# Two 512-channel gates ahead of the dilated queries and keys in a hybrid decoder layer

## The chip, the cores and the metric

The kernel runs on one core of one Trainium2 chip. The metric is the device time of one execution in microseconds. Three runs of the kernel before took 474.70, 476.15 and 476.85 us, so the median is 476.15 us.

## What is computed

One post-norm decoder layer for 256 positions of 1024 channels, all in float32. The mixer projects x once into MoBA q, k, v, dilated q, k, v, the three inputs of a short convolution, and three gates; each branch is projected back, weighted by its sigmoid gate and summed:

```python
qa, ka, va, qd, kd, vd, b_gate, c_gate, hc, gate_logits = jnp.split(x @ w_in, split_points, axis=-1)
y_moba = moba_attention(heads(qa, MOBA_HEADS), heads(ka, MOBA_HEADS), heads(va, MOBA_HEADS))
y_conv = b_gate * causal_dwconv(c_gate * hc, w_short_conv)
y_dil = dilated_mixture(heads(qd, DIL_HEADS), heads(kd, DIL_HEADS), heads(vd, DIL_HEADS))
gates = jax.nn.sigmoid(gate_logits).reshape(b, s, N_BRANCH, D_MODEL)
merged = (gates[:, :, 0] * (y_moba @ w_moba_proj)
          + gates[:, :, 1] * (y_conv @ w_conv_proj)
          + gates[:, :, 2] * (y_dil @ w_dil_proj))
return merged @ w_mix_out
```

Behind it come a layer norm, a SwiGLU MLP whose up-projection passes a causal convolution of width 3, and a second layer norm. `w_in` is 1024 x 8448: 768 columns each for dilated q, k and v, and 1024 columns for each of the three gates.

## The kernel before

**Weights.** All weight blocks stand in one list, `blocks`, in the order of their use. A block is 1 MB (128 partitions x 2048 floats) and lands in one of `RAW` = 3 buffers `raw`, by DMAs on SP's queue. `prep` takes the next quarter of a block (a *piece*, 128x512), and `split` makes two operands of it: ScalarE (ACT) casts it to fp32r (L168, or L160 in the first stage), and VectorE (DVE) subtracts that from the original (L169). When the last piece of a block is split, the next block's DMA is issued. Pieces may be made up to `LEAD` = 10 ahead of use; they lie in a pool `b` of 61 buffers, which serves nearly all other intermediate tiles too.

**Products.** `mm3` makes each product of three fp32r matmuls (L229, L230, L231). `project` makes 256 channels as two halves of 128 channels x 256 positions: the weight is loaded, x streams, 24 matmuls of 256 columns a half, and the result lies in one of three PSUM banks `acc`. `by_tokens` makes 512 channels for the two halves of positions: x is loaded, the weight streams, 48 matmuls of 512 columns into two `acc` banks. `tick` runs between: it makes further pieces, hands the finished bank to its consumer (`queries`, `keys`, a sigmoid), and takes one step from the list `side`, in which the attention's steps and `small_weights` wait. Each engine's instructions run in the order written by a scheduler.

**The first stage.** `first_products` runs while x and the first two blocks arrive, one 128-row step k at a time, with transposes of x (L222) between; it makes the queries of dilated groups 0 and 1 (four accumulators, 96 matmuls of 256 columns, L499). Then come the queries of group 2 and the keys of all three groups (`project`), dilated v, and the rest: MoBA, the short convolution, and, for each half d of the 1024 channels, three gates by `by_tokens` with a sigmoid (L580) and the merge of the three branches.

**The small rows.** `small_loads` fetches the convolution weights and bias as rows of 128 floats (12 rows, and 4 x 44 rows). `small_weights` turns them with five PE transposes (L484, L486) into one PSUM tile and copies them out on DVE (L487, L488). It is the fifth entry of `side` while the keys are projected. The short convolution reads `sconv` first, behind the dilated v and the MoBA v; `fconv` is for the MLP.

Of the kernel before, what the change touches and what calls it, by code (L numbers as in the profile page):

```python
# [7 lines left out]
F32 = mybir.dt.float32  # L8
# [3 lines left out]
AF = mybir.ActivationFunctionType  # L12
OP = mybir.AluOpType

P = 128
T = 256
D = 1024
KT = D // P
# [8 lines left out]
DIL_Q, DIL_K, DIL_V = 1536, 2304, 3072  # L27
CONV_B, CONV_C, CONV_H = 3840, 4352, 4864
GATE = 5376
# [8 lines left out]
def trunk(ctx: ExitStack, tc, x, w_in, w_short_conv, w_moba_proj, w_dil_proj, w_conv_proj, w_mix_out,  # L38
          ln1_g, ln1_b, w_up, w_ffn_conv, b_ffn_conv, w_down, ln2_g, ln2_b, out):
    nc = tc.nc  # L40
# [12 lines left out]
    def fresh(name):  # L53
        serial[0] += 1
        return f"{name}{serial[0]}"

    def buf(dt=F32, shape=(P, 512)):
        return act.tile(list(shape), dt, tag="b2", name=fresh("b"), bufs=B2)

    def acc(shape=(P, 512)):  # L60
        return ps.tile(list(shape), F32, tag="acc", name=fresh("acc"), bufs=3)
# [8 lines left out]
    def block(*parts):  # L70

        blocks.append(parts)

    def kview(w, c0, c1, k0=0, k1=None):
        k1 = w.shape[0] // P if k1 is None else k1
        return w[k0 * P:k1 * P, c0:c1].rearrange("(k p) c -> p k c", p=P)

    def columns(base, n):
        for b in range(n):
            c = base + 256 * b  # L80
            block(kview(w_in, c, c + 256))

    def wide(base):

        for k in (0, 4):
            block(kview(w_in, base, base + 512, k, k + 4))

    for k in (0, 4):
        block(kview(w_in, DIL_Q, DIL_Q + 512, k, k + 4))
    columns(DIL_Q + 512, 1)  # L90
    columns(DIL_K, 3)
    wide(DIL_V)
    columns(DIL_V + 512, 1)
# [6 lines left out]
    columns(CONV_B, 2)  # L100
    for c in range(0, D, 512):
        for g in range(3):
            wide(GATE + g * D + c)
        block(kview(w_dil_proj, c, c + 512), kview(w_conv_proj, c, c + 512, 0, 2))
        block(kview(w_conv_proj, c, c + 512, 2, 4), kview(w_moba_proj, c, c + 512, 0, 2))
        block(kview(w_moba_proj, c, c + 512, 2, 4))
# [12 lines left out]
    def load_next(between=None):  # L119
        i = len(loads)  # L120
        if i >= len(blocks):
            return
        r = act.tile([P, 2048], F32, tag="raw", name=fresh("raw"), bufs=RAW)
        at = 0
        for p in blocks[i]:
            k, c = p.shape[1:]
            step = 1 if i < 2 else 2 if i == 2 else k
            for k0 in range(0, k, step):
                if between:
                    between(i * 4 + k0)  # L130
                n = step * c
                loading[0] = nc.sync.dma_start(r[:, at:at + n].rearrange("p (k c) -> p k c", c=c), p[:, k0:k0 + step, :])
                at += n
        loads.append(r)
        pieces.extend((r, c, c + 512 == at) for c in range(0, at, 512))

    def prep(n=1):

        for _ in range(n):
            i = len(ready)  # L140
            if i >= min(len(pieces), used[0] + LEAD):
                return
            r, c, last = pieces[i]
            h, l = buf(F32R), buf(F32R)
            split(r[:, c:c + 512], h, l)
            ready.append((h, l))
            if last:
                load_next()

    def take(n):  # L150

        i = used[0]
        assert len(ready) >= i + n, (len(ready), i, n)
        return ready[i:i + n]

    def behind(last, f, *args):
        if last is None:
            return f(*args)
        with tc.issue_after(last.ins):
            return f(*args)  # L160
# [3 lines left out]
    def split(src, h, l):  # L164
        if in_order:
            in_order[0] = behind(in_order[0], nc.scalar.copy, h, src)
        else:
            nc.scalar.copy(h, src)  # L168
        nc.vector.tensor_sub(l, src, h.bitcast(F32))  # L169


    side, late = [], []

    def tick(n, consume=None, ahead=1):


        used[0] += n
        while late:
            late.pop(0)()
        prep(n + ahead)  # L180
        if consume:
            consume()
        if side:
            side.pop(0)()
# [22 lines left out]
    for i in range(RAW):  # L207
        load_next(load_x if i < 2 else None)
# [18 lines left out]
    def mm3(o, ah, al, bh, bl, first, last):  # L227

        nc.tensor.matmul(o, ah, bh, start=first, stop=False)  # L229
        nc.tensor.matmul(o, ah, bl, start=False, stop=False)  # L230
        nc.tensor.matmul(o, al, bh, start=False, stop=last)  # L231
# [15 lines left out]
    def by_tokens(xs, n, consume, ahead=1):  # L247


        o = [acc() for _ in range(2)]  # L250
        for k in range(0, n, 2):
            w = take(2)
            for i in range(2):
                xh, xl = xs(k + i)
                for t in range(2):
                    s = slice(t * P, (t + 1) * P)
                    mm3(o[t], xh[:, s], xl[:, s], *w[i], k + i == 0, k + i == n - 1)
            tick(2, (lambda: [consume(t, o[t]) for t in range(2)]) if k == n - 2 else None, ahead)
# [30 lines left out]
    def queries(store):  # L289

        def consume(c, o):
            q = buf(F32R, (P, 2, T))
            for a in range(2):
                s = HALF[a]
                nc.scalar.copy(q[s, a, :], o[s, :])
            for a in range(2):
                s, n = HALF[a], HALF[1 - a]
                nc.vector.tensor_sub(q[n, a, :], o[s, :], q.bitcast(F32)[s, a, :])  # L298
            store.append(q)
        return consume  # L300
# [145 lines left out]
    def both(*fs):  # L446
        return lambda: [f() for f in fs]
# [41 lines left out]


    dq, dk, dv = [[], [], []], [[], [], []], []
    o = [(acc if c < 2 else att)((P, T)) for c in range(4)]

    def first_products(k, part):

        w = ready[k]
        xt, i = ((xTh, 0), (xTl, 0), (xTh, 1))[part]
        for c in range(4):
            last = nc.tensor.matmul(o[c], w[i][:, c * P:c * P + P], xt[:, k, :], start=k + part == 0,  # L499
                                    stop=k == KT - 1 and i == 1)  # L500
        if part == 2:
            used[0] += 1
            prep(1 if used[0] > 4 else 0)
        return last

    turns = {(0, 0): ((0, 1), (1, 2)), (1, 0): ((2, 4),), (3, 0): ((4, 6),), (5, 0): ((6, 8),)}
    last = None
    for k in range(KT):
        for part in range(3):
            for k0, k1 in turns.get((k, part), ()):  # L510
                last = behind(last, transpose_x, k0, k1)
                prep(k1 - k0)
            if k + part == 0:
                last = behind(last, warmed, 2, 256)
            last = behind(last, first_products, k, part)
    in_order.clear()
    for g in range(2):
        q = queries(dq[g])
        for c in range(2):
            q(c, o[2 * g + c])  # L520
            prep()
    for g in range(2, 3):
        project(queries(dq[g]), ahead=0)
    small_loads()
    side += [lambda: None] * 4 + [small_weights]
    for g in range(3):
        project(keys(dk[g]), ahead=0)
    assert not side
    yd = [buf(F32R, (P, 2, T)) for _ in range(2)]
    p, q = (dilated(c, dq, dk, dv, [t[:, c, :] for t in yd]) for c in range(2))  # L530
    side += [p[0], p[1], p[2], q[0], p[3], p[4], q[1], p[5], q[2], p[6], q[3], q[4], q[5], q[6]]
    dv.extend(project_tokens())
    dv.append(project_tokens_half())
    mv = project_tokens()
# [3 lines left out]
    for b in range(2):  # L538
# [21 lines left out]
        p, q = (moba(c, mq, mk, mv[b], [t[:, c, :] for t in ym]) for c in range(2))  # L560
# [15 lines left out]
    for d in range(2):  # L576
        gs = []
        for g in range(3):
            s = [buf(F32), buf(F32)]
            by_tokens(of_x, KT, lambda t, o: nc.scalar.activation(s[t], o, AF.Sigmoid))  # L580
            gs.append(s)
        assert not side
        h, l = ([buf(F32R, (P, 2, T)) for _ in range(2)] for _ in range(2))

        def turn_m(t, gs=gs, h=h, l=l):
            p = att((P, 4, P))
            for i in range(4):
                nc.tensor.transpose(p[:, i, :], gs[2][t][:, i * P:(i + 1) * P], ident)  # L588
            for i in range(2):
                split(p[:, 2 * i:2 * i + 2, :], h[i][:, :, t * P:(t + 1) * P], l[i][:, :, t * P:(t + 1) * P])  # L590

        for g, n, ys in ((2, 2, [yd]), (1, 4, ycT), (0, 4, ymT)):

            def merge(t, o):
                nc.vector.tensor_mul(gs[g][t], o, gs[g][t])
                if g < 2:
                    nc.vector.tensor_add(gs[2][t], gs[2][t], gs[g][t])

            by_tokens(lambda k: [y[:, k % 2, :] for y in ys[k // 2]], n, merge)
        side += [lambda f=turn_m: f(0), lambda f=turn_m: f(1)]  # L600
        merged.extend(zip(h, l))
# [69 lines left out]
    w = take(4)  # L671
# [16 lines left out]
    def between():  # L688
        passed.append(prep(1))
        if len(passed) == 2:  # L690
            turn_x1(0, 0)
            turn_x1(0, 1)
# [29 lines left out]
    w = take(8)  # L722
    u = []
    for t in range(2):
        o = acc()
        s = slice(t * P, (t + 1) * P)
# [23 lines left out]
    for j in range(2, NJ, 2):  # L750
# [3 lines left out]
        while 2 < j < NJ - 2 and pend:  # L754
            w = take(4)
# [49 lines left out]
```

## Time and profile before

| what | value |
|---|---|
| median of 3 runs | 476.15 us |
| the profiled execution | 475.9 us, of which 474.1 us span |
| TensorE (PE) busy | 463.7 us (98%) |
| VectorE (DVE) busy | 355.5 us (75%) |
| ScalarE (ACT) busy | 268.4 us (57%) |
| mean granted TensorE clock | 0.992 |
| moved by DMA | 83.45 MB, 176 GB/s |

The span is cut into 40 slices in the profile's second part; a busy TensorE there is a sequence of pipelined matmuls, whose rate is read from the distance of their starts, not from their durations. The granted clock is given as a share of 2.4 GHz.

### The profile page before, as it was taken

To read this page: it belongs to the slowest core of one execution; us is meant where nothing else is said; L and a number is where in the kernel's file an instruction comes from. 1 tells how busy PE (TensorE), PEld (TensorE's weight loads), DVE (VectorE), ACT (ScalarE), POOL (GpSimd) and SP (SyncE) were. 2 spreads that over 40 slices of the span, in tenths; PEclk is the share of its full clock that TensorE was granted. 3 is DMA by queue.
4 is the path that set the end of the run, shared out by engine and by line. 5 is a ranking of instruction groups with operands and counts; after the bars stand their busy time and mean duration, and the time that the engine had idled before them with its cause. 6 is when DMAs were issued, how large, how long until landed. Compare 5 with 4: busy or idle time off the path is not lost.

```text
span 474.1 us, 8155 instructions
## 1 busy us (share of the span) xinstructions
PE 463.7 (98%) x3095; PEld 426.3 (90%) x3095; DVE 355.5 (75%) x756; ACT 268.4 (57%) x568; POOL 10.4 (2%) x29
## 2 busy tenths in 40 slices
PE   8989999999999999999999999999999999999993
PEld 6989898999999888888888899999999999999983
DVE  5895998678989944775477966997767686786866
ACT  4894585736667844634463325876565565664710
POOL 1100000010100000000000000000000000000000
PEclk9998999999999999999999999999999999999998
DMA  8963665653544654646554804557455646637202
GB/s 283 325 205 105 197 183 176 224 178 90 178 130 138 187 201 168 220 159 207 191 211 146 266 1 154 201 179 267 157 199 178 198 157 205 225 107 248 105 1 88
DMA packets 57739, 83.45 MB, mean 176 GB/s; under 512 B 1705, under 2 KB 41317, under 8 KB 57701
## 3 DMA queue, kind: packets, MB, share of 16 engines
q1 hardware_dynamic: 57700, 82.94, 52.7%
q8 instruction: 24, 0.39, 0.4%
q14 instruction: 15, 0.11, 0.1%
HBM read 81.89 MB, written 1.05 MB: 175 GB/s over the span
## 4 chain that ended last, share of the span: by engine, by line
PE 94%; DMA 2%; DVE 2%; issue 1%; SPq 0%; ACT 0%; DVEq 0%
PE acc L229 23%; PE acc L231 22%; PE acc L230 22%; PE att L230 7%; PE att L229 7%; PE att L231 7%; PE att L326 2%; PE att L347 1%; DMA b<-in_w_ffn_conv_dram 1%; PE acc L499 1%; PE att L499 1%; DMA xs<-in_x_dram 1%; DVE b L169 1%; DVE b L298 0%; PE att L588 0%
## 5 line engine op out<-in xcount | busy, mean ns | idle before, releaser
L169 DVE TENSOR_TENSOR b<-raw,b 128x512 fp32r<-128x512 f32 x300 | 194.0, 686 | 41.6 <-ACT b L168 38.7
L168 ACT CAST b<-raw 128x512 fp32r<-128x512 f32 x288 | 160.2, 619 | 2.4 <-DMA raw<-in_w_up_dram 2.1
L229 PE MATMUL acc<-x1Th,b 128*128 128x256 f32 x320 | 90.9, 284 | 0.0
L231 PE MATMUL acc<-x1Th,b 128*128 128x256 f32 x320 | 90.6, 283 | 0.0
L230 PE MATMUL acc<-x1Tl,b 128*128 128x256 f32 x320 | 90.5, 283 | 0.0
L229 PE MATMUL acc<-xTh,b 128*128 128x256 f32 x224 | 64.8, 289 | 0.4 <-DVE b L298 0.4
L230 PE MATMUL acc<-xTl,b 128*128 128x256 f32 x224 | 63.9, 285 | 0.0
L231 PE MATMUL acc<-xTh,b 128*128 128x256 f32 x224 | 63.9, 285 | 0.0
L230 PEld LDWEIGHTS acc<-x1Tl,b 128*128 128x128 f32 x320 | 61.4, 192 | 0.1
L229 PEld LDWEIGHTS acc<-x1Th,b 128*128 128x128 f32 x320 | 61.4, 192 | 0.1
L231 PEld LDWEIGHTS acc<-x1Th,b 128*128 128x128 f32 x320 | 61.4, 192 | 0.0
L702 DVE SCALAR_TENSOR_TENSOR b<-acc,fconv,b 128x255 f32<-128x255 f32 x80 | 38.3, 479 | 30.3 <-ACT b L700 29.3
L229 PE MATMUL att<-b,b 128*128 128x512 f32 (+1 forms) x170 | 59.1, 348 | 0.0
L230 PE MATMUL att<-b,b 128*128 128x512 f32 (+1 forms) x170 | 58.9, 347 | 0.0
L231 PE MATMUL att<-b,b 128*128 128x512 f32 (+1 forms) x170 | 58.7, 346 | 0.0
L229 PE MATMUL acc<-b,xTh 128*128 128x512 f32 (+1 forms) x144 | 54.7, 381 | 0.0
L230 PE MATMUL acc<-b,xTh 128*128 128x512 f32 (+1 forms) x144 | 54.4, 378 | 0.0
L231 PE MATMUL acc<-b,xTl 128*128 128x512 f32 (+1 forms) x144 | 54.4, 378 | 0.0
L229 PEld LDWEIGHTS acc<-xTh,b 128*128 128x128 f32 x224 | 43.6, 194 | 0.8 <-PE acc L231 0.6
L230 PEld LDWEIGHTS acc<-xTl,b 128*128 128x128 f32 x224 | 43.6, 195 | 0.0
L231 PEld LDWEIGHTS acc<-xTh,b 128*128 128x128 f32 x224 | 43.5, 194 | 0.0
L700 ACT ACTIVATE b<-acc,fconv 128x256 f32<-128x256 f32 x40 | 22.6, 564 | 28.7 <-PE acc L231 28.6
(118 smaller groups left out, 649.2 us busy)
## 6 DMA issues: line engine op xcount, KB each, us to landing
raw<-in_w_in_dram SPq DMA_DIRECT2D x30, 1024.0 KB, 5.4
raw<-in_w_up_dram SPq DMA_DIRECT2D x22, 1024.0 KB, 5.2
raw<-in_w_down_dram SPq DMA_DIRECT2D x11, 1024.0 KB, 5.0
raw<-in_w_mix_out_dram SPq DMA_DIRECT2D x4, 1024.0 KB, 4.9
raw<-in_w_in_dram SPq DMA_DIRECT2D x12, 256.0 KB, 5.5
raw<-in_w_conv_proj_dram SPq DMA_DIRECT2D x4, 512.0 KB, 4.8
raw<-in_w_moba_proj_dram SPq DMA_DIRECT2D x4, 512.0 KB, 5.1
xs<-in_x_dram SPq DMA_DIRECT2D x4, 256.0 KB, 4.9
```

Source lines behind the costliest of these rows:

```text
L168: nc.scalar.copy(h, src)
L169: nc.vector.tensor_sub(l, src, h.bitcast(F32))
L229: nc.tensor.matmul(o, ah, bh, start=first, stop=False)
L230: nc.tensor.matmul(o, ah, bl, start=False, stop=False)
L231: nc.tensor.matmul(o, al, bh, start=False, stop=last)
L326: nc.tensor.matmul(o, qt, k[i][:, a, :], start=i == 0, stop=i == 1)
L347: nc.tensor.transpose(p[:, i, :], b, ident)
L499: last = nc.tensor.matmul(o[c], w[i][:, c * P:c * P + P], xt[:, k, :], start=k + part == 0, stop=k == KT - 1 and i == 1)
L700: nc.scalar.activation(v, o, AF.Identity, bias=w[3], scale=w[0])
L702: nc.vector.scalar_tensor_tensor(v[:, j:], o[:, :T - j], w[j], v[:, j:], op0=OP.mult, op1=OP.add)
```

## The change

The first stage makes 512 channels of gate 2, by tokens, in place of the queries of groups 0 and 1. Gate 1 (512 channels) follows, then all three groups of queries, then the keys. The four sigmoid tiles of the two gates are kept in the pool `b` until the merge of d = 0, which then projects gate 0 alone. `small_weights` goes from the keys to the ninth step of the dilated attention. Blocks 2 and 3 come as two DMAs each.

```diff
-    for k in (0, 4):
-        block(kview(w_in, DIL_Q, DIL_Q + 512, k, k + 4))
-    columns(DIL_Q + 512, 1)
+    EARLY = (2, 1)
+    for g in EARLY:
+        wide(GATE + g * D)
+    columns(DIL_Q, 3)
     columns(DIL_K, 3)
...
         for g in range(3):
-            wide(GATE + g * D + c)
+            if c or g not in EARLY:
+                wide(GATE + g * D + c)
...
-            step = 1 if i < 2 else 2 if i == 2 else k
+            step = 1 if i < 2 else 2 if i < 4 else k
...
-    o = [(acc if c < 2 else att)((P, T)) for c in range(4)]
+    o = [acc() for _ in range(2)]
...
-        for c in range(4):
-            last = nc.tensor.matmul(o[c], w[i][:, c * P:c * P + P], xt[:, k, :], start=k + part == 0,
+        for t in range(2):
+            last = nc.tensor.matmul(o[t], xt[:, k, t * P:(t + 1) * P], w[i], start=k + part == 0,
...
-    for g in range(2):
-        q = queries(dq[g])
-        for c in range(2):
-            q(c, o[2 * g + c])
-            prep()
-    for g in range(2, 3):
+    gates0 = {}
+
+    def gate_into(s):
+        return lambda t, o: nc.scalar.activation(s[t], o, AF.Sigmoid)
+
+    for g in EARLY:
+        s = gates0[g] = [buf(F32), buf(F32)]
+        if g == EARLY[0]:
+            for t in range(2):
+                gate_into(s)(t, o[t])
+        else:
+            by_tokens(of_x, KT, gate_into(s))
+    for g in range(3):
         project(queries(dq[g]), ahead=0)
     small_loads()
-    side += [lambda: None] * 4 + [small_weights]
...
-    side += [p[0], p[1], p[2], q[0], p[3], p[4], q[1], p[5], q[2], p[6], q[3], q[4], q[5], q[6]]
+    side += [p[0], p[1], p[2], q[0], p[3], p[4], q[1], p[5], both(q[2], small_weights), p[6], q[3], q[4], q[5], q[6]]
...
+            if d == 0 and g in EARLY:
+                gs.append(gates0[g])
+                continue
```

Lines of `first_products` and behind it stand two or more further down in the changed kernel: L229 to L231 become L231 to L233, L484 and L486 become L486 and L488, the sigmoid's L580 becomes L522.

On PE, before, this is the place where the last key's half of group 1 ends (`acc_512`) and the small rows (`b_114`, `b_115`) are turned, with two matmuls of the first attention scores (`att_728`) between:

```order
L231 MATMUL acc_512<-xTh,b_409 128x256
L484 MATMUL att_643<-ident,b_114 128x12
L486 MATMUL att_643<-ident,b_115 128x44
L326 MATMUL att_728<-b_457,b_303 128x256
L486 MATMUL att_643<-ident,b_115 128x44
L326 MATMUL att_728<-b_458,b_303 128x256
L486 MATMUL att_643<-ident,b_115 128x44
L229 MATMUL acc_555<-xTh,b_366 128x256
```

In the changed kernel the same transposes stand on PE between two k-steps of the MoBA v projection (`acc_1179`, `acc_1180`), in one group:

```order
L233 MATMUL acc_1180<-b_1021,xTl 128x512
L486 MATMUL att_1297<-ident,b_112 128x12
L488 MATMUL att_1297<-ident,b_113 128x44 x4
L231 MATMUL acc_1179<-b_1085,xTh 128x512
L232 MATMUL acc_1179<-b_1086,xTh 128x512
```

They moved behind 12 halves of queries and keys, the dilated v and three steps of the MoBA v.

On ACT, before, the end of the first stage: the last turned x, five pieces (`raw_81`, `raw_88`), then the first queries out of PSUM, with a piece (`raw_167`) behind each:

```order
L160 CAST xTh<-att_236 128x512
L160 CAST b_243<-raw_81 128x512
L160 CAST b_249<-raw_88 128x512
L160 CAST b_265<-raw_88 128x512
L160 CAST b_281<-raw_88 128x512
L160 CAST b_297<-raw_88 128x512
L295 CAST b_303<-acc_116 64x256 x2
L168 CAST b_308<-raw_167 128x512
L295 CAST b_312<-acc_117 64x256 x2
```

On ACT, in the changed kernel, at the same place:

```order
L162 CAST xTh<-att_203 128x512
L162 CAST b_210<-raw_81 128x512
L162 CAST b_216<-raw_88 128x512
L162 CAST b_226<-raw_88 128x512
L162 CAST b_236<-raw_88 128x512
L162 CAST b_246<-raw_88 128x512
L522 ACT_TABLE_LOAD
L522 ACTIVATE b_252<-acc_114 128x512
L522 ACTIVATE b_253<-acc_115 128x512
L170 CAST b_272<-raw_157 128x512
```

A table load and two sigmoids have taken the place of the queries' casts. A further table load stands ahead of the first exponentials, so there are five in all, where there were three.

On PE, in the changed kernel, the end of the first stage (gate 2 in `acc_114`, `acc_115`) and the start of gate 1, whose second tile `acc_259` takes the bank of `acc_114`:

```order
L501 MATMUL acc_114<-b_211,xTh 128x512
L501 MATMUL acc_115<-b_211,xTh 128x512
L231 MATMUL acc_258<-b_216,xTh 128x512
L232 MATMUL acc_258<-b_217,xTh 128x512
L233 MATMUL acc_258<-b_216,xTl 128x512
L231 MATMUL acc_259<-b_216,xTh 128x512
```

Before, the queries of group 2 began here, in the third bank alone.

## Rows read from the trace of the kernel before

**Rows 1.** The page: busy time, share of the span and instructions of PE, and the granted clock in 40 slices (tenths).

```profile
PE 463.7 (98%) x3095; PEld 426.3 (90%) x3095; DVE 355.5 (75%) x756; ACT 268.4 (57%) x568; POOL 10.4 (2%) x29
PEclk9998999999999999999999999999999999999998
```

**Rows 2.** Busy time of each engine by stretch: from:to, length, then PE, PEld, DVE, ACT, POOL busy (instructions), granted clock, DMA share, GB/s. The first row is the first stage; the next four lie in the queries and keys, then the dilated attention, then the gates of d = 0.

```profile
5.33:18.63 13.30, 13.17 (x109) 12.97 (x110) 9.59 (x16) 7.96 (x16) 1.23 (x4) 1.00 1.00 329
...
27.27:27.87 0.60, 0.15 (x2) 0.03 (x1) 0.56 (x3) 0.58 (x2) 0.00 (x0) 1.00 0.74 167
27.87:33.70 5.83, 5.83 (x48) 5.78 (x48) 5.63 (x11) 5.44 (x12) 0.00 (x0) 1.00 0.99 342
33.70:36.51 2.81, 1.71 (x9) 0.96 (x7) 2.72 (x6) 2.14 (x5) 0.00 (x0) 0.92 0.48 116
36.51:43.70 7.19, 7.19 (x49) 7.11 (x48) 2.04 (x5) 2.15 (x5) 0.00 (x0) 0.79 0.32 111
...
46.92:80.00 33.08, 33.08 (x205) 29.71 (x204) 32.68 (x90) 23.35 (x52) 0.00 (x0) 1.00 0.59 184
170.00:190.00 20.00, 20.00 (x90) 16.57 (x89) 9.81 (x16) 9.75 (x19) 0.00 (x0) 1.00 0.53 178
```

**Rows 3.** Starts of matmuls on PE (start us, duration, engine, line, operands): the first stage at step k = 1 and at its last transposes of x; the first and last matmul of 72 of 256 columns (one record is missing); the first of the dilated v; and two of 40 matmuls of 512 columns in the gates.

```profile
7.15 0.66 PE L222 MATMUL att<-ident,xs 128*128 128x128 f32 x4
7.56 0.48 PE L499 MATMUL acc<-xTh,b 128*128 128x256 f32 x2
...
13.88 0.60 PE L222 MATMUL att<-ident,xs 128*128 128x128 f32 x4
...
18.63 0.28 PE L229 MATMUL acc<-xTh,b 128*128 128x256 f32 x1
...
27.15 0.28 PE L231 MATMUL acc<-xTh,b 128*128 128x256 f32 x1
...
46.92 0.40 PE L229 MATMUL acc<-b,xTh 128*128 128x512 f32 x1
...
181.69 0.39 PE L229 MATMUL acc<-b,xTh 128*128 128x512 f32 x1
...
190.53 0.39 PE L229 MATMUL acc<-b,xTh 128*128 128x512 f32 x1
```

**Rows 4.** Who waited for whom, longest first (total us, times, longest): 26 to 48 us, and one wait of the first 60 us.

```profile
DVE sconv L487 <- PE att L486: 5.4, 1, 5.4
...
PE att L486 <- DMA b<-in_w_ffn_conv_dram: 1.1, 2, 0.6
PE acc L229 <- DVE b L298: 0.4, 1, 0.4
...
PEld att L222 <- DMA xs<-in_x_dram: 0.3, 1, 0.3
```

**Rows 5.** PE in order of time, 33.5 to 37 us.

```profile
33.79 0.23 PE L484 MATMUL att<-ident,b 12*128 12x12 f32 x1
34.52 0.26 PE L486 MATMUL att<-ident,b 44*128 44x44 f32 x1 [0.50 <-DMA b<-in_w_ffn_conv_dram]
...
35.69 0.26 PE L486 MATMUL att<-ident,b 44*128 44x44 f32 x1 [0.61 <-DMA b<-in_w_ffn_conv_dram]
...
36.24 0.33 PE L486 MATMUL att<-ident,b 44*128 44x44 f32 x1
36.51 0.58 PE L229 MATMUL acc<-xTh,b 128*128 128x256 f32 x1
```

**Rows 6.** Busy time of each engine in one stretch, columns as in Rows 2.

```profile
36.00:38.00 2.00, 2.00 (x9) 1.74 (x10) 1.93 (x5) 0.07 (x1) 0.00 (x0) 0.52 1.03 354
```

**Rows 7.** The chain of work that ended last, in order of time (start us, us, what): a group of four transposes of x, and the rows' transfer.

```profile
14.04 0.44 PE att L222 x4
30.01 5.63 DMA b<-in_w_ffn_conv_dram
```

**Rows 8.** PE in order of time, around the fifth transpose of the small rows.

```profile
43.55 0.28 PE L231 MATMUL acc<-xTh,b 128*128 128x256 f32 x1
43.76 0.26 PE L486 MATMUL att<-ident,b 44*128 44x44 f32 x1
43.95 0.38 PE L229 MATMUL acc<-xTh,b 128*128 128x256 f32 x1
```

**Rows 9.** ACT in order of time: the end of the first stage, and the table load ahead of the first Silu; then the sigmoids of the gates (durations min/median/max in ns).

```profile
14.51 0.59 ACT L160 CAST xTh<-att 128x512 fp32r<-128x512 f32 x1 [1.19 <-PE att L222]
14.99 2.70 ACT L160 CAST b<-raw 128x512 fp32r<-128x512 f32 x5
...
296.65 1.28 ACT L711 ACT_TABLE_LOAD   x1
297.95 0.73 ACT L711 ACTIVATE b<-b 128x256 f32<-128x256 f32 x2
...
L580 ACT ACTIVATE b<-acc x12: 598/598/599, 169.0 to 238.7; 128x512 f32<-128x512 f32 x12
```

**Rows 10.** DVE's instructions of the pieces (the page: busy us, mean ns, idle before) and of the keys (min/median/max ns).

```profile
L169 DVE TENSOR_TENSOR b<-raw,b 128x512 fp32r<-128x512 f32 x300 | 194.0, 686 | 41.6 <-ACT b L168 38.7
...
L317 DVE CAST b<-acc x5: 417/418/419, 31.3 to 47.7; 64x256 fp32r<-64x256 f32 x5
...
L318 DVE TENSOR_TENSOR b<-acc,b x8: 416/422/428, 31.7 to 46.0; 64x256 fp32r<-64x256 f32 x8
```

More of the change, by code (lines that the diff above doesn't have):

```diff
@@ L578, in trunk @@
         for g in range(3):
+            if d == 0 and g in EARLY:
+                gs.append(gates0[g])
+                continue
             s = [buf(F32), buf(F32)]
-            by_tokens(of_x, KT, lambda t, o: nc.scalar.activation(s[t], o, AF.Sigmoid))
+            by_tokens(of_x, KT, gate_into(s))
             gs.append(s)
```

## The prediction

> **What bounds the kernel now.** I read the page first. TensorE (PE) is busy 98% of the span, and its granted clock is at nine tenths or more in every slice but the fourth (35.6 to 47.4 us) and the last [rows 1]. So the change can only win what PE loses by waiting, by a lower clock, or by matmuls that disappear. None disappears here: the same products are made in another order. The next view is busy time by stretch [rows 2]. In the gates (170 to 190 us) PE has no gap at all, and in the dilated attention (46.92 to 80 us) it has none either, though DVE is busy there for 32.68 of 33.08 us. The loss lies between the first stage and 46.92 us, so that stretch is what I cost.
>
> The ruler is the distance between starts [rows 3]: from 18.63 to 27.15 us there are 71 steps of 256-column matmuls, 0.120 us each; from 181.69 to 190.53 us 39 steps of 512 columns, 0.227 us each. Between 18.63 us, where the first stage's last matmul has been started, and 46.92 us, where dilated v begins [rows 3], stand 28.29 us. The work in it is eight halves of 24 matmuls, 192 x 0.120 = 23.04 us, and two score matmuls, 0.24 us. So 5.01 us are lost, and the stretches say where [rows 2]:
> - 27.27 to 27.87 us, 0.60: PE waits for a PSUM bank that DVE has still to empty (L298) [rows 4].
> - 33.70 to 36.51 us, 2.81 less 0.24 for the scores = 2.57: the small rows are turned while they are still on their way [rows 4]. PE stands twice before L486, until the transfer lands [rows 5].
> - 36.51 to 43.70 us, 7.19 for 48 matmuls that need 5.76 = 1.43: the clock. The granted clock was 0.52 between 36 and 38 us [rows 6], that is the lower of its two levels, 1.2 GHz, right behind that waiting.
> - the rest, 0.41, is the fifth transpose and restarts.
>
> **The change, part by part.** *The first stage.* It takes 13.30 us now [rows 2], for 96 matmuls of 256 columns, three groups of transposes of x and one wait for x [rows 4]. With the gate it has 48 of 512 columns, 6 x 0.227 = 1.36 us a step of k. Step 0 runs from 5.33 to 6.69 us; the transposes for step 1 wait for x until 7.15, as now, and step 1 starts at 7.56 [rows 3]. Four steps and a group of transposes (0.44 us [rows 7]) put the last transposes at 13.45 us (now 13.88 [rows 3]); three more steps and that group end the stage at 17.98: 12.65 us. The gate of 48 x 0.227 = 10.90 us leaves the later stage, and 96 x 0.120 = 11.52 us of queries are added in `project`. (12.65 + 11.52) - (13.30 + 10.90) = -0.03. The exchange is worth nothing by itself. Gate 1 moves whole: nothing.
>
> *The bank wait at 27.27 us.* It goes. Now the four query tiles finish together at 18.6 us, and DVE takes eight subtractions of 0.42 us behind the first stage's pieces. In the change the gates leave PSUM through ACT alone, and DVE has 10.9 us of matmuls for the 12 pieces that follow, 12 x 0.686 = 8.2 us [rows 10]. It then meets the keys without a backlog. There, a half of 2.88 us of matmuls gives DVE two pieces, one cast and two subtractions: 1.37 + 0.42 + 0.84 = 2.63 us [rows 10]. That fits by 0.25 us only; if it doesn't, waits of 0.60 come back (first rival). The queries need 2.2 us.
>
> *The small rows.* Their five DMAs stay on SP's queue, behind the keys' blocks, and are issued before the keys are done; they took 5.63 us from issue to use [rows 7]. The order shows the transposes behind all twelve halves, dilated v and part of the MoBA v, some 50 us of matmuls. So the wait goes, and with it the slow clock. What stays is the work: four transposes in a group cost 0.44 us [rows 7], one alone 0.40 - 0.12 = 0.28 us [rows 8]. Five cost between 0.55 (one group) and 1.40 (apart); the order has them in one group, so 0.55. DVE also stood for 5.4 us before `sconv`, L487 [rows 4], with the pieces queued behind it; that time comes back to DVE ahead of the stretch in which it is nearly full [rows 2], which makes a new wait there less likely than now.
>
> *The table loads.* ACT gets two more. One is covered: it runs before the first exponentials, and PE has the other dilated v steps until it needs them. The other stands between the pieces and the first sigmoid, and gate 1's second tile needs the bank that this sigmoid empties. The last cast of x starts at 14.51 us and five piece casts end at 17.69 [rows 9]; with the transposes 0.43 us earlier they end at 17.26. A load took 1.28 us and the next activation began 0.02 later [rows 9]: 18.56. The sigmoid takes 0.60 [rows 9]: 19.16. PE ends the stage at 17.98 and has three matmuls for the free bank, until 18.66. New wait: 0.50 us. Its bounds are 0 (ACT gets to the load earlier than I think) and 1.9 (it is late by another load's length). Behind the sigmoids on ACT stand the pieces 12 and on, needed 5.4 us of matmuls later: covered.
>
> The Trainium skill's page "ScalarE: Activation LUTs", section "What ACT_TABLE_LOAD costs", counts 2.66 us a switch, the load and a drain of 1.38. The trace agrees with the load and shows no drain [rows 9]. By the page the wait would be about 1.9 us and the time 473.4.
>
> *The rest.* Four sigmoid tiles and two row tiles stay long in the pool of 61. In the built order three piece splits of the attention now wait for a matmul, where none did; from that matmul to the first use of the piece stand 25 to 30 us of matmuls. Nothing, then. The merge of d = 0 follows the MoBA after one gate instead of three; 10.9 us of cover are left, in a stage in which DVE works half the time [rows 2]. Nothing. Two DMAs each for blocks 2 and 3: before, five DMAs for the two, so SP issues one less. Nothing.
>
> **The sum.** 5.01 - 0.55 - 0.50 + 0.03 = 3.99 us less. The profiled execution took 475.9 us, so 471.9; that run was 0.25 below the median of 476.15, and I say 472.0.
>
> **The rivals.**
> 1. *Queries and keys still wait.* DVE has a margin of 0.25 us per half, and one slip gives back 0.60, as at 27.27 us; two give 473.2. For it: DVE was full from 20 us on. Against it: the backlog came from the four tiles at once, and they are gone.
> 2. *The bank wait at 18.7 us is long and takes the clock with it.* If it is 1.9 us and the clock falls behind it as at 36 us, 1.4 + 1.43 is lost: 474.8. For it: the longer wait by rows 5 was followed by the low clock. Against it: 0.60 us at 27.27 was followed by full clock [rows 2].
> 3. *The change doesn't do what it says:* the rows are late again at their new place. Then 2.57 - 0.55 and 1.43 stay lost: about 475.5. Against it: 50 us of matmuls ahead.
> 4. *Slower: the pool runs out.* Splits that wait for a free tile hold ACT, and behind them on ACT stand the exponentials and the emptying of PSUM. It decides from the point where the lead of 25 us is used up. Each such gap costs what the only long one of this trace did, 2.3 + 1.43 = 3.7 us; with two of them the time is 479.4. For it: six tiles of 61 are gone in the fullest stage, and such waits appear in the order. Against it: the 25 us.
>
> **How the numbers follow.** Forecast 0.62 (470.1 to 473.4); rival 1 0.10; rival 2 0.12; rival 3 0.06; rival 4 0.10. The range goes from 470.1 (no bank wait, 0.5, and as far below as the fastest run of before lies under its median, 1.4) to 475.5, which takes in rivals 1 and 2. A change of 0.5%, 2.4 us, is about what three runs that spread by 2.15 us can tell, so "faster" is below 473.8: 0.62 and nearly all of rival 1, 0.71. Same: rivals 2 and 3 and the edge, 0.19. Slower: rival 4, 0.10.
>
> **What would show it.** Right: the first stage ends near 18.0 us; one PE wait for a sigmoid of about 0.5 us near 18.7; no granted clock below 1.00 between 18 and 64 us; dilated v starts near 46.92 + 21.80 - 4.5 = 64.2 us (two gates more, the loss less the transposes); five transposes together near 105 us without a wait. Wrong: any PE wait for DVE among the keys (rival 1), a slice of low clock behind 19 us (rival 2), a wait at L488 for a DMA (rival 3), or PE waits for pieces between 64 and 120 us (rival 4).

## The result, and the profile after

The change makes the kernel 0.5% faster: 473.13 us (median of 6, 472.96 to 474.44) against 476.10 (median of 6, 474.26 to 476.85) for the kernel before, ratio 0.995 with a 95% interval from 0.993 to 0.997. The execution that was profiled is the slowest of the six, 474.44 us. Busy time and clock on its page:

```profile
PE 463.2 (98%) x3095; PEld 425.4 (90%) x3095; DVE 355.3 (75%) x756; ACT 270.8 (57%) x570; POOL 10.3 (2%) x29
...
PEclk9999999999999999999999999999999999999998
```

Against [rows 1], TensorE does the same work, and the slice with the low clock (35.6 to 47.4 us) is gone. ACT has two instructions and 2.4 us more, the two table loads. Its waits of PE, longest first (total us, times, longest):

```profile
PE acc L195 <- DVE warm L190: 1.2, 1, 1.2
PE acc L231 <- ACT b L522: 0.4, 1, 0.4
PE att L224 <- DMA xs<-in_x_dram: 0.2, 1, 0.2
```

That is the whole list. The first stands in the kernel before too, ahead of the warm-up. Of [rows 4] the wait for the small rows (L486 there) and the one for DVE's subtractions (L298) have gone; the one for a sigmoid is new. By stretch, columns as in [rows 2]:

```profile
18.00:26.00 8.00, 7.63 (x33) 5.95 (x33) 6.20 (x12) 7.87 (x14) 0.00 (x0) 1.00 0.86 265
...
34.00:42.00 8.00, 8.00 (x69) 8.00 (x68) 5.29 (x11) 5.19 (x12) 1.22 (x4) 1.00 0.66 214
...
58.00:66.00 8.00, 8.00 (x69) 8.00 (x68) 7.05 (x15) 6.23 (x15) 0.00 (x0) 1.00 0.71 243
```

From 26 us to the end of the keys PE has no gap, and the clock is full. PE and then ACT at the end of the first stage (start, duration, what; the brackets hold the idle time ahead and what ended it):

```profile
20.11 0.39 PE L231 MATMUL acc<-b,xTh 128*128 128x512 f32 x1
...
20.56 0.39 PE L233 MATMUL acc<-b,xTl 128*128 128x512 f32 x1
21.32 0.51 PE L231 MATMUL acc<-b,xTh 128*128 128x512 f32 x1 [0.37 <-ACT b L522]
```

```profile
16.65 2.70 ACT L162 CAST b<-raw 128x512 fp32r<-128x512 f32 x5
19.37 1.28 ACT L522 ACT_TABLE_LOAD   x1
20.67 1.08 ACT L522 ACTIVATE b<-acc 128x512 f32<-128x512 f32 x2
```

Five piece casts, the load, then the sigmoid whose end lets PE go on. PE starts 21.32 - 20.56 - 0.23 = 0.53 us late (0.227 is the distance of such starts, [rows 3]). The small rows are turned much later, between two matmuls of the MoBA v:

```profile
101.82 0.39 PE L233 MATMUL acc<-b,xTl 128*128 128x512 f32 x1
102.14 0.23 PE L486 MATMUL att<-ident,b 12*128 12x12 f32 x1
102.30 0.44 PE L488 MATMUL att<-ident,b 44*128 44x44 f32 x4
102.67 0.50 PE L231 MATMUL acc<-b,xTh 128*128 128x512 f32 x1
```

No wait, and 102.67 - 101.82 - 0.23 = 0.62 us for all five, against 2.57 in the stretch of [rows 5].

### The profile page after: what moved, and what is told of

Read it like the earlier page. It is cut to its first block, busy times and chain, and to the rows that moved or that the text cites. A ratio compares the mean times of both kernels' runs of the same rounds, so it can differ in the third digit from the quotient of the medians.

```text
span 472.6 us, 8159 instructions
## 1 busy us (share of the span) xinstructions
PE 463.2 (98%) x3095; PEld 425.4 (90%) x3095; DVE 355.3 (75%) x756; ACT 270.8 (57%) x570; POOL 10.3 (2%) x29
## 4 chain that ended last, share of the span: by engine, by line
PE 96%; ACT 1%; DMA 1%; DVE 1%; issue 0%; DVEq 0%; ACTq 0%
PE acc L231 23%; PE acc L233 23%; PE acc L232 23%; PE att L231 7%; PE att L233 7%; PE att L232 7%; PE att L328 2%; PE acc L501 2%; PE att L349 1%; DMA xs<-in_x_dram 1%; ACT b L162 1%; PE att L224 1%; PE att L599 0%; ACT L522 0%; DVE r L634 0%
## 5 line engine op out<-in xcount | busy, mean ns | idle before, releaser
L231 PE MATMUL acc<-x1Th,b 128*128 128x256 f32 x320 | 91.0, 284 | 0.0
L233 PE MATMUL acc<-x1Th,b 128*128 128x256 f32 x320 | 90.7, 283 | 0.0
L231 PE MATMUL acc<-xTh,b 128*128 128x256 f32 x256 | 72.9, 285 | 0.0
L232 PE MATMUL acc<-xTl,b 128*128 128x256 f32 x256 | 72.5, 283 | 0.0
L233 PE MATMUL acc<-xTh,b 128*128 128x256 f32 x256 | 72.5, 283 | 0.0
L231 PEld LDWEIGHTS acc<-x1Th,b 128*128 128x128 f32 x320 | 61.4, 192 | 0.1
L233 PEld LDWEIGHTS acc<-x1Th,b 128*128 128x128 f32 x320 | 61.5, 192 | 0.0
L231 PE MATMUL att<-b,b 128*128 128x512 f32 (+1 forms) x170 | 59.2, 348 | 0.0
L233 PE MATMUL att<-b,b 128*128 128x512 f32 (+1 forms) x170 | 58.8, 346 | 0.0
L231 PE MATMUL acc<-b,xTh 128*128 128x512 f32 (+1 forms) x128 | 48.9, 382 | 0.4 <-ACT b L522 0.4
L232 PEld LDWEIGHTS acc<-xTl,b 128*128 128x128 f32 x256 | 49.1, 192 | 0.1
L231 PEld LDWEIGHTS acc<-xTh,b 128*128 128x128 f32 x256 | 49.1, 192 | 0.1
L233 PEld LDWEIGHTS acc<-xTh,b 128*128 128x128 f32 x256 | 49.1, 192 | 0.0
L232 PE MATMUL acc<-b,xTh 128*128 128x512 f32 (+1 forms) x128 | 48.3, 377 | 0.0
L233 PE MATMUL acc<-b,xTl 128*128 128x512 f32 (+1 forms) x128 | 48.2, 377 | 0.0
```

## Experiments

Two questions were open. Which part of the change earns the gain? And why is the gain 3 us, where the sum said 4? The kernel before was run again beside the others each time; a ratio is always to it, on the same chip.

**The small rows later, and nothing else.** In the kernel before:

```diff
-    side += [lambda: None] * 4 + [small_weights]
...
-    side += [p[0], p[1], p[2], q[0], p[3], p[4], q[1], p[5], q[2], p[6], q[3], q[4], q[5], q[6]]
+    side += [p[0], p[1], p[2], q[0], p[3], p[4], q[1], p[5], both(q[2], small_weights), p[6], q[3], q[4], q[5], q[6]]
```

> The kernel before, with the small rows turned as late as in the change (the ninth step of the dilated attention) and the queries still first. Theory: the loss was the wait for the small rows (2.57 us less 0.55 of work that stays) and the slow clock behind it (1.43 us), so this alone gives most of the gain: 3.0 to 3.8 us less than before, and no granted clock below 1.00 between 30 and 47 us; the wait of 0.6 us near 27.3 us stays, and one or two more of its kind may come in the keys, where ACT and DVE are still behind. Rival: the early gates are what frees ACT and DVE, and without them the keys wait for banks: less than 1.5 us gained.

472.74 us, ratio 0.9952 (0.9934 to 0.9969), 1.96 us under before's median of 474.70 on that chip and not the 3.0 to 3.8 expected. The clock is full from 16 to 50 us, as the theory had it. Its waits of PE, beside the one ahead of the warm-up:

```profile
PE acc L229 <- DVE b L298: 0.4, 1, 0.4
PE acc L499 <- ACT b L160: 0.3, 1, 0.3
```

**The gates first, and nothing else.** The changed kernel, with the small rows back at their step among the keys:

```diff
+    side += [lambda: None] * 4 + [small_weights]
...
-    side += [p[0], p[1], p[2], q[0], p[3], p[4], q[1], p[5], both(q[2], small_weights), p[6], q[3], q[4], q[5], q[6]]
+    side += [p[0], p[1], p[2], q[0], p[3], p[4], q[1], p[5], q[2], p[6], q[3], q[4], q[5], q[6]]
```

> The changed kernel, with the small rows turned at their old step among the keys. Theory: the rows were late because SP issued their transfers behind weight blocks that waited for a DVE with a backlog; with the gates first there is no backlog, the rows are issued near 50 us and turned near 60 us, so PE does not wait, and the time is that of the changed kernel within 0.5 us. Rival: the later place is needed, PE waits for the transfer as before and the clock falls: 2 to 3.5 us more than the changed kernel.

472.58 us, ratio 0.9954 (0.9936 to 0.9973): the theory holds, the rival falls. One wait of PE is left in the whole run, beside the one ahead of the warm-up:

```profile
PE acc L231 <- ACT b L522: 0.4, 1, 0.4
```

**The changed kernel, beside these two.**

> The changed kernel once more, for its time on this chip and for a second profile of its start. Theory: the profiled run of the changed kernel (474.44 us) was 1.3 us above its median because the matmuls of its first step ran at half rate (0.43 us each for 512 columns) until 9.2 us; a run at the median has them at 0.23 us from step 0 or 1 on, and its first stage ends near 18.8 us instead of 20.1. Rival: the first stage always ends near 20 us, and the difference of the runs comes from another place.

472.70 us, ratio 0.9954 (0.9937 to 0.9970), and the first stage ends at 18.50, as the theory had it. So each part alone earns all of it, and both together earn no more. The reason is in the two lists. Either part takes the rows' wait away: the later step by itself, or the gates. For the gates, SP's queue and PE's order show how. In the kernel before, SP issues the first of the rows' DMAs at 26.09 us, then a weight block (L132) that has waited for its buffer, then the others; the block and the last of the rows:

```profile
29.08 0.38 SPq L132 DMA_DIRECT2D raw<-in_w_in_dram  x1
...
30.78 0.35 SPq L479 DMA_DIRECT2D b<-in_b_ffn_conv_dram  x1
```

With the gates first, the first and the last of the rows, and PE's first transpose of them:

```profile
48.23 0.50 SPq L478 DMA_DIRECT2D b<-in_w_short_conv_dram  x1
...
49.91 0.35 SPq L481 DMA_DIRECT2D b<-in_b_ffn_conv_dram  x1
...
61.99 0.23 PE L486 MATMUL att<-ident,b 12*128 12x12 f32 x1
```

Before, PE comes to the rows 3 us after the last DMA (30.78, then 33.79 in [rows 5]), behind three halves of keys. With the gates first the five DMAs are issued without a block between, and PE comes to the rows 12 us after the last, behind five halves. Where the gates do it, the wait for DVE (L298) goes too, but a wait for ACT (L522) of the same size takes its place. PE in this execution: step 1 of the first stage, its end, and the first of the dilated v:

```profile
7.73 0.70 PE L501 MATMUL acc<-b,xTh 128*128 128x512 f32 x2
8.27 0.63 PE L501 MATMUL acc<-b,xTl 128*128 128x512 f32 x2
8.74 1.16 PE L501 MATMUL acc<-b,xTh 128*128 128x512 f32 x4
...
18.50 0.39 PE L231 MATMUL acc<-b,xTh 128*128 128x512 f32 x1
...
18.95 0.39 PE L233 MATMUL acc<-b,xTl 128*128 128x512 f32 x1
19.73 0.50 PE L231 MATMUL acc<-b,xTh 128*128 128x512 f32 x1 [0.39 <-ACT b L522]
...
64.61 0.40 PE L231 MATMUL acc<-b,xTh 128*128 128x512 f32 x1
```

The stage ends at 18.50 and the wait costs 0.55. From 19.73 to 64.61 us PE has no wait that the profile names.

**The table load ahead of everything.** The changed kernel, with one sigmoid of one column behind the warm-up:

```diff
     warmed(WARM, 512)
+    first_set = const.tile([P, 1], F32, name="first_set")
+    nc.scalar.activation(first_set, warm[:, 0:1], AF.Sigmoid)
```

> The changed kernel, with a sigmoid of one column ahead of everything on ACT, so that the sigmoid's table is the first that is loaded and no load stands between the pieces and the first gate. Theory: the wait of PE for the bank of gate 1's second tile (0.37 us idle, 0.53 us late) goes: 0.4 to 0.6 us less than the changed kernel. Rival: PE has that time back elsewhere (the casts of x start later, or another wait takes its place): within 0.2 us.

472.33 us, ratio 0.9946 (0.9927 to 0.9966), 0.37 under the changed kernel on that chip (by the means of all executions 0.44). ACT, then PE:

```profile
0.72 1.28 ACT L201 ACT_TABLE_LOAD   x1 [0.72 <-PEq L806]
...
18.79 1.09 ACT L525 ACTIVATE b<-acc 128x512 f32<-128x512 f32 x2 [0.69 <-PE acc L504]
```

```profile
19.27 0.39 PE L236 MATMUL acc<-b,xTl 128*128 128x512 f32 x1
19.50 0.45 PE L234 MATMUL acc<-b,xTh 128*128 128x512 f32 x1
```

Now ACT waits for PE, and PE for nothing. The load was the whole of the new wait.

**One gate instead of two.** The changed kernel with

```diff
-    EARLY = (2, 1)
+    EARLY = (2,)
```

> The changed kernel with gate 2 alone ahead of the queries; gate 1 goes back to the merge. Theory: ten microseconds of work that DVE need not empty are enough to clear the backlog, and behind the first gate stands a projection that uses the one free bank for 2.9 us, so the table load and the sigmoid are covered: PE waits for nothing between 18 and 55 us, and the time is 0.3 to 0.5 us less than the changed kernel's. Rival: one gate leaves ACT and DVE behind in the queries, and waits of 0.4 to 0.6 us for L297 to L320 come back: the same time or more.

472.53 us, ratio 0.9940 (0.9919 to 0.9962). Whether that is the 0.3 to 0.5 less that was expected can't be told, since the changed kernel was not run on that chip. The load stands where it stood on ACT, but the queries that follow gate 2 find a free bank. PE goes straight on, and no wait of PE is named behind it:

```profile
18.11 0.61 PE L501 MATMUL acc<-b,xTh 128*128 128x512 f32 x2
18.56 0.28 PE L231 MATMUL acc<-xTh,b 128*128 128x256 f32 x1
```

**Both of these.** One gate, and the load ahead.

> One early gate, and the sigmoid's table loaded ahead of everything. Theory: the load is covered already with one gate, so this takes the time of the one-gate kernel within 0.2 us. Rival: ACT is late for the pieces there too, and the load's 1.28 us still count: 0.3 us less.

472.42 us, ratio 0.9936 (0.9914 to 0.9959), on the chip of the run with one gate. The load is worth 0.1 where it is covered, which these runs do not tell from nothing, and 0.37 where it is not.

**The kernel before, unchanged.** Is its profile typical?

> The kernel before once more, for a second profile. Theory: PE waits for the small rows as in the first profile (about 2 us near 34 us); the granted clock behind it falls or not, and the mean clock of the run tells which: at 0.992 or 0.993 the 48 matmuls behind take 7.2 us and the run takes 475.5 or more, at 0.995 and above they take 5.8 to 6.2 us and the run 473.6 to 475. Rival: the clock falls in every run, and the runs differ in the length of the wait.

475.38 us, ratio 1.0001 (0.9981 to 1.0020). But the execution that was profiled, 474.23 us, is not the one of [rows 5]. PE (the end of the first stage, the rows' place, the first of the dilated v), its longest wait between the first two, and the clock from 36 to 38 us:

```profile
18.40 0.28 PE L229 MATMUL acc<-xTh,b 128*128 128x256 f32 x1
...
34.25 0.23 PE L484 MATMUL att<-ident,b 12*128 12x12 f32 x1
34.95 0.26 PE L486 MATMUL att<-ident,b 44*128 44x44 f32 x1 [0.48 <-DMA b<-in_w_ffn_conv_dram]
...
36.14 0.39 PE L229 MATMUL acc<-xTh,b 128*128 128x256 f32 x1
...
45.25 0.40 PE L229 MATMUL acc<-b,xTh 128*128 128x512 f32 x1
```

```profile
PE acc L229 <- DVE b L298: 1.1, 1, 1.1
```

```profile
36.00:38.00 2.00, 2.00 (x17) 1.95 (x17) 1.96 (x5) 0.53 (x2) 0.00 (x0) 1.00 0.89 290
```

PE waited once for the rows, 0.48, and behind it the clock is full; in [rows 6] the same two microseconds had 0.52, and 9 matmuls instead of 17. The bank wait (L298) is longer than in the first profile, 1.1 instead of 0.4, so the sizes of both waits change from one execution to the next. The mean granted clock of each execution tells how often the clock falls: the low stretches of [rows 2] take (0.08 x 2.81 + 0.21 x 7.19)/474 = 0.004 off it, which is the distance between 0.992 and 0.996. In the comparisons with the kernel before, those at a mean of 0.993 or less against the rest:

| kernel | executions | at 0.993 or less | their mean time | the others' |
|---|---|---|---|---|
| before, chip A | 16 | 6 | 476.01 | 474.26 |
| before, chip B (8 of them in this experiment) | 31 | 9 | 476.19 | 475.09 |
| before, chip C | 14 | 3 | 476.45 | 474.00 |
| eight kernels in which PE doesn't wait for the rows | 69 | 0 | | |

The last row is the changed kernel and the seven others here without that wait, on the chips A to C and in the first comparison. So the kernel before is at the lower mean in 18 executions of 61, at 1.1 to 2.5 us each. The execution of [rows 6] was of that kind too (0.992); none of the 18 was profiled, so that their clock fell at the same place is inferred. Chip A ran the first four experiments, chip B the next four (one gate, both, this one and the wait filled), chip C the last two.

The clock is not all of it. At 0.995 and above 473.6 to 475 us was expected here; four of those seven executions took 475.14 to 477.00. On chip A the two kinds do not overlap (475.01 at most, 475.54 at least), on chip B they do.

**The wait filled with work.** In the kernel before, ten bf16 matmuls whose result nobody reads, ahead of the transposes; built so, these came two halves later.

```diff
         n = 2 * NJ
+        for _ in range(10):
+            nc.tensor.matmul(p, warm[:, :P], warm, start=True, stop=True)
         nc.tensor.transpose(p[:, 0:12], row1[0:12], ident[0:12, 0:12])
```

> The kernel before, with ten bf16 matmuls of 512 columns (2.3 us) on PE ahead of the small rows' transposes, where it waited before; the order then puts the transposes two halves of keys later. Theory: part of the kernel before's spread (473.6 to 476.5 us) is the clock, which falls behind the wait in some executions and costs 1.4 us there; with matmuls in place of the wait PE loses as long, but the clock stays, so all runs lie near the faster half of the kernel before, 473.5 to 474.5 us, with a spread under 1.2 us. Rival: the spread comes from the start of the kernel: it stays near 3 us, with runs above 475.5.

474.78 us (12 executions), ratio 0.9994 (0.9978 to 1.0010). PE at the place where the rows were waited for:

```profile
33.96 0.28 PE L231 MATMUL acc<-xTh,b 128*128 128x256 f32 x1
34.30 2.10 PE L485 MATMUL att<-warm 128*128 128x512 bf16 x9
36.06 0.47 PE L229 MATMUL acc<-xTh,b 128*128 128x256 f32 x1
```

From 33.96 to 36.06 the useful matmuls stand still for about as long as before, and none of the 12 executions lost its clock (0.995 at least). The time is not what the theory said: the median lies above 473.5 to 474.5, and the spread is 2.3 us, not under 1.2, with two executions of 476.46 and 476.65 at a clock of 0.996. So the rival has a part in it: on this chip something beside the clock makes some executions about 2 us longer. The mean, 475.00, is 0.38 under that of before's 23 executions in this comparison, 475.38, and by those the clock would make 8/23 x (476.18 - 474.96) = 0.42. The two agree, but the interval of the ratio takes in 1, so what the clock alone is worth is not shown by this run.

**The wait doubled.** In the kernel before, four more row transfers ahead of the rows:

```diff
     def small_loads():
+        for j in range(4):
+            nc.sync.dma_start(row2[64:64 + 2 * NJ, j, :], w_ffn_conv[j % 3].rearrange("(t c) -> t c", c=P))
```

> The kernel before with four more row transfers on SP's queue ahead of the rows that the transposes need (into a part of the tile that nothing reads), so that PE's wait in front of L486 is longer by some four issues of about 0.5 us: 2 us, now 0.5 to 1.1 us, expected 2.5 to 3. Theory (the clock falls behind the rows' wait, and whether it does so hangs on how long that wait is): it now falls in nearly every execution, mean granted clock at or under 0.993 in all of them, and the time is above before's by the 2.0 us of wait and, in the two thirds of executions in which before kept its clock, by 1.4 to 1.75 more: median 478.5 to 479. Rival (the fall is a chance of its own, about one execution in three, whatever the length of the wait): two groups of executions as in before, median about 2 us above before's, 477.4 to 478. Second rival (the wait costs nothing that the end sees): same as before.

476.92 us (5 executions) against 474.09, ratio 1.0049 (1.0014 to 1.0083). Three of five had a clock of 0.990 to 0.993 and took 476.92 to 478.65; the other two 474.95 and 475.22. The one profiled is of the latter kind:

```profile
33.64 0.28 PE L231 MATMUL acc<-xTh,b 128*128 128x256 f32 x1
35.95 0.23 PE L486 MATMUL att<-ident,b 12*128 12x12 f32 x1 [2.03 <-DMA b<-in_w_short_conv_dram]
```

```profile
36.00:38.00 2.00, 2.00 (x12) 1.62 (x13) 1.93 (x6) 0.13 (x1) 0.00 (x0) 1.00 0.56 161
```

A wait of 2.03 us, nearly twice the two of [rows 5] together (0.50 and 0.61), where 2.5 to 3 was expected, and the clock stayed full behind it. So the theory that the length of the wait alone decides falls; the fall is a matter of the execution. The rival's median of 477.4 to 478 did not come either: within each kind the longer wait costs 1.1 to 1.3 us (475.09 against 474.00, 477.70 against 476.45, by the means). Whether a longer wait makes it likelier, three in five against 18 in 61, five executions can't tell.

**A longer warm-up.** The changed kernel with `WARM = 8` instead of 6.

> The changed kernel with eight warm-up matmuls of 512 columns ahead of the first transposes of x instead of six. Theory (the first step's half rate, 0.43 us a matmul in the profiles in which it showed, comes of a clock that is not up yet when x lands, and a longer warm-up covers it where x lands late): profile without a matmul of 0.4 us or more apart in the first step, first stage done by 18.5, time 0 to 0.5 us under the changed kernel's, 472.3 to 472.7. Rival (the warm-up is long enough, and two more only stand in front of the transposes): first stage later by up to 0.4 us, 472.7 to 473.1.

473.17 us (10 executions), ratio 0.9975 (0.9960 to 0.9991) on that chip; the changed kernel's own ratio elsewhere is 0.9954. Part of that distance is before's clock, which fell less often on this chip; against before's executions that kept it, this kernel's mean is 0.8 us less here, the changed kernel's 1.5 on chip A. The first stage, PE:

```profile
4.57 1.06 PE L224 MATMUL att<-ident,xs 128*128 128x128 f32 x4
...
6.18 1.17 PE L501 MATMUL acc<-b,xTh 128*128 128x512 f32 x2
7.18 0.62 PE L501 MATMUL acc<-b,xTl 128*128 128x512 f32 x2
```

The two more stand in front of the transposes (4.57, where the run of the changed kernel above had them at 3.71), and the first product begins at 6.18 instead of 5.35. Only the first pair stands apart at the slow pace (1.00, where the pair had 0.56 above). The first stage ends at 19.24, not by 18.5, so the theory falls. The time is near the rival's 472.7 to 473.1; that the longer warm-up takes more in front of the transposes than it brings is likely and not shown, since the changed kernel was not run on this chip and x does not land at the same time in every execution (the changed kernel's first profile has its transposes at 4.14).

## Why the prediction was right, and which terms were off

Forecast 472.0 us in a range from 470.1 to 475.5; measured 473.13, and 472.70 on chip A. The mechanisms came as forecast. Its gain was 4.1 us and the measured one 3.0 or 2.0, and that is worked out here.

*The bank wait and the small rows.* Right that both go: neither wait is in the changed kernel. In the last stretch of the keys DVE is busy 7.05 of 8.00 us, 0.88; the step said 2.63 of 2.88, 0.91, and no half slipped (rival 1). The transposes cost 0.62 us, said 0.55. The prediction did not ask which part of the change the rows need; either does it. For the gates by themselves its terms leave 0.60 + 0.03 - 0.50 = 0.13 us once the rows are out of the way, and no gain shows: the means on chip A are 472.65 with the rows alone and 472.77 with both.

*The new wait.* Right in place and cause: 0.53 and 0.55 us, said 0.50. It ends with the first sigmoid, which starts 0.02 us behind the load (19.37 + 1.28 = 20.65, then 20.67). The Trainium skill's page "ScalarE: Activation LUTs", section "What ACT_TABLE_LOAD costs", adds a drain of 1.38 us; the trace again shows none. Both ends of this difference came late: in the changed kernel's second profile the load starts at 17.79, said 17.26, and the stage ends at 18.50, said 17.98. Both stand behind the last transposes of x, so the difference held. The clock did not fall behind this wait in any execution counted (rival 2).

*The stall of the pool (rival 4).* The list names no wait of PE between 21.32 us and the end, so the lead of the pieces was enough.

*The clock, 1.43.* Mis-sized as a gain. The step read it from one execution and took it as the kernel's. It belongs to 6 of 16 executions on chip A, where it is worth 1.75: 6/16 x 1.75 = 0.66 on average. The three times known before the prediction, 474.70, 476.15 and 476.85, lie 1.4 to 2.2 apart, as these two kinds of execution do. The prediction took that spread as the noise of the measurement. For the time forecast it did no harm: the sum starts from the very execution that had lost its clock, 475.9.

*The first stage, -0.03.* Mis-sized, and most of what put 472.0 too low. The side before was measured, the side after was computed from the pitch of the gates, 0.227, where no transposes interrupt. In the execution above, 7.73 to 18.50 is 10.77 us for 42 matmuls and two groups of transposes, where 42 x 0.227 + 2 x 0.44 = 10.41 was said: the first two matmuls behind a group take 0.54 together (7.73 to 8.27) instead of 0.45, the next two 0.47. Step 1 also began 0.17 later, since x landed so. The stage ended at 18.50 instead of 17.98. The end of this stage moves from one execution to the next: in the five profiles with the first stage of before it lies between 18.40 and 19.16, in those with the gate and the same warm-up between 18.50 and 18.92, and once at 20.11. In none does it come at 17.98.

With the two profiles at full clock, that of before in these experiments (474.23) and that of the changed kernel (473.02), the sum can be done again. Before: from 18.40, the end of the first stage, to 45.25, the dilated v, 26.85 us stand for 23.28 of work, 3.57 lost. The prediction has 5.01 less the clock's 1.43, 3.58; that the two agree so closely is luck, since the waits within are not the same (the bank's is 1.1 here). After: from 18.50 to 64.61, 46.11 for 10.90 + 12 x 2.88 = 45.46, 0.65 lost. The transposes take 0.62. The first stage costs 0.72: queries of 11.52 us have left it and a gate of 10.90 has come, so it should end 0.62 earlier to come out even, and it ends 0.10 later. The gain is 3.57 - 0.65 - 0.62 - 0.72 = 1.58. On chip A the executions above 0.993 give 474.26 - 472.76 = 1.50; with 0.66 for the clock that makes 2.16, which is what the means of all executions there differ by, 474.92 - 472.76. The pair itself, which comes from two chips, differs by 1.21 only; the other 0.37 is lost behind the start of the dilated v, where the sum has only the transposes, 0.27 of it in one step of the changed kernel's second profile (263.55 to 264.05 us) that its first does not have. The cause stays open.

In the first comparison the difference is 3.0. Four of before's six times lie above 476, and on chip A only executions at the lower mean do. The clock of these six is not on record (the profiled execution, 475.9 us at 0.992, is a seventh), and on chip B some at full clock take as long, so that the clock made the 3.0 is inferred. If so, it is luck that the gain came out as near to 4.1 as it did: with the median of chip A it is 2.0. The changed kernel's profile there is 1.3 us above its median, and its first stage ends at 20.11, which the last section shows.

*Open:* why an execution keeps or loses its clock behind the same wait, and what makes some of them on chip B longer at full clock.

**What does better.** One gate, with the table load at the start, is 472.42 at a ratio of 0.9936, and two gates with the load at the start 0.9946; the changed kernel's is 0.9954. Their intervals overlap, and the first stands on another chip than the other two. The trace no longer has the 0.55 us of wait; that the time gains 0.1% by it is likely and not shown.

## What to carry to other kernels

A loss that one profile shows may belong to some executions only: put the mean granted clock beside each time first, and count a clock that falls by how often it does. When a stretch before is measured and the one after is computed from a clean pitch, the restarts are missing on one side. And when two edits remove the same wait, try each alone: here moving one step of the program earned as much as the whole change.

## What the runs showed of the hardware that was not expected

In the profiled execution of the change the first step ran at half its pace. PE, then the stretch's row (clock behind the counts):

```profile
5.78 1.22 PE L501 MATMUL acc<-b,xTh 128*128 128x512 f32 x2
6.80 1.05 PE L501 MATMUL acc<-b,xTl 128*128 128x512 f32 x2
7.66 1.05 PE L501 MATMUL acc<-b,xTh 128*128 128x512 f32 x2
8.51 1.06 PE L224 MATMUL att<-ident,xs 128*128 128x128 f32 x4
```

```profile
6.00:10.00 4.00, 4.00 (x13) 3.24 (x14) 1.39 (x3) 1.02 (x3) 0.00 (x0) 1.00 1.02 368
```

Two matmuls take 0.86 us (6.80 to 7.66) instead of 0.46, and the granted clock reads 1.00 all the same. The step takes 2.73 us (5.78 to 8.51), where six matmuls at 0.227 are 1.36, and so costs this execution about as much as it lies above its median, 1.3. With the table load ahead the first two pairs were slow too; with the longer warm-up only the first (6.18 to 7.18), in the changed kernel's second profile none. The change does not bring it: with the first stage of before and the small rows later, pairs of 256-column matmuls start 0.43 apart there (6.12, 6.55) instead of 0.24. Half the pace is what the lower clock level would give, but the row doesn't show that level, and the cause stays open.
